# A gated DeltaNet and Conformer block: two sigmoids queued behind a rounding, and decay exponentials moved up in ScalarE's order

## The chip, the cores and the metric

The kernel runs on one core of one Trainium2 chip. The metric is the device time of one execution in microseconds (us). Each engine of the core (TensorE for matrix products, VectorE, ScalarE, GpSimd, and SyncE, which here issues the loads) works through a stream of instructions of its own in a fixed order; engines wait for one another by semaphores. In the profile they are called PE, DVE, ACT, POOL and SP, in that order; DMA is the transfer of data to and from HBM.

## The reference, cut to what matters

The block takes x of 512 tokens by 1024 channels, in float32. What lies around the change is the start:

```python
h = rmsnorm(x, norm1_w)
proj = h @ w_in                       # q, k, v, z, b, a, glu, gates
beta = sigmoid(b);  g = -exp(A_log) * softplus(a + dt_bias)
qkv = silu(causal_depthwise_conv(qkv, dn_conv_w))      # 4 taps
# per head and chunk of 64 tokens: gc = cumsum(g)
decay = exp(where(tril, gc[i] - gc[j], -inf))          # used twice per head
t_mat = eye + where(strict, beta[i] * (k @ k.T) * decay, 0)
attn = (q @ k.T) * decay
ga, gb = split(glu + b_glu);  c = ga * sigmoid(gb)     # then a 31-tap convolution
```

Behind that come the triangular solves and the recurrence over chunks, the merging of both mixers by sigmoid gates, a SwiGLU channel mixer and a last RMSNorm.

## The kernel before

**Tiling.** Channels lie on 128 partitions, tokens (512) along a row. A projection `proj(j)` (L397) gives 128 output channels: one weight unit of 128 x 1024 is loaded, ScalarE rounds it into `whi` (L113), VectorE subtracts to get the rest `wlo` (L115), and TensorE makes 8 x 3 products of 128 x 512 (L124): `whi` with `hh`, `whi` with `hl`, `wlo` with `hh`, where `hh` and `hl` are the rounded part and the rest of the normalized input, in 8 slices k. Raw weights, `whi` and `wlo` have three buffers each.

**The start.** While the norm is not yet known, the products of the first two pairs of gated units (win rows 40, 32, 41, 33) are made from the unnormalized input (L264 to L324). `normalized(k)` (L337) then makes slice k: VectorE scales `xt`, ScalarE rounds to `hh[k]` (L340), VectorE subtracts to `hl[k]` (L341). `glu0(i)` (L323) scales the early products, and its inner function `gated` does the sigmoid on ScalarE (L332) and the gating product on VectorE (L333). The small chain for g and beta stands between, with two Exp (L363, L364) and a Ln (L366). The first projections that use all 8 slices are those of k and q of head 0, interleaved (`proj2`, L408); so TensorE needs `hh[7]` and `hl[7]` last.

**The decays.** `decays` (L792) makes the cumulated sums of g on TensorE (L798), writes them to HBM (`mrow`, L809), and `masked` (L442) reads for each head a row broadcast into a tile `DT` (L446) and adds the triangular mask on GpSimd (L448). There are four `DT` buffers. `decay` (L453) then does four Exp of 128 x 128 for each head on ScalarE (L458). It is called in heads 0, 1, 3 and 5, for the heads (0, 1), (2, 3), (4, 5) and (6, 7). Users of a `DT` are `Un` x `DT` on GpSimd (L485) and `at` on VectorE (L523).

**What sets the order.** Each engine's stream is laid out when the program is built, by a list planner with a model of time: when an engine of the model falls free, it takes, of the instructions whose inputs and buffers are ready, the one with the lowest number. An instruction's number is the value of a counter (`tc.cur_priority`) that goes up by one with each instruction that the Python code emits. `tc.issue_after(i)` adds an order edge, only for instructions on the same engine as `i`, and no wait for `i` to end. In `decay` the first `issue_after` names a GpSimd instruction, so it binds no Exp; for the first call, `silu[0]` does. Activation-table loads (`ACT_TABLE_LOAD` in the profile) are not written by hand; they stand where the next function needs another table.

Counted through the code, ScalarE's instructions around the change have these numbers: Exp of the decays of heads 0 and 1 436 to 443; the copy that starts `y` (L504) 465; rounding of units 24, 42, 34, 9, 1, 17 (L113) 497, 525, 574, 589, 621, 653, of head 2's k, q and v 909, 957, 997; Silu of z (L844) 523; the four scalings of `Vp` (L518) 543 to 546; four squares (L526) from 556; the sigmoid of the third gated unit (L684) 572; Exp of the decays of heads 2 and 3 661 to 668; of heads 4 and 5 1397 to 1404; of heads 6 and 7 2164 to 2171. `hh[7]` (L340) has 274, the Ln (L366) 263, the two sigmoids (L332) 279 and 281. The masks of heads 2 and 3 on GpSimd (L448) have 445 and 447, `Un` x `DT` of head 0 (L485) 448. Unit 9 is k of head 1, the next projection behind unit 34.

Of the kernel before, what the change touches and what calls it, by code (L numbers as in the profile page):

```python
# [9 lines left out]
AF = mybir.ActivationFunctionType  # L10
# [14 lines left out]
START = 78  # L25
ROUND = 40
WARM = 9
OTHERS = (12, 12, 12, 12, 8, 8, 8, 8)
EPS = 1e-6

# [2 lines left out]
def block_kernel(ctx, tc, a):  # L33
    nc = tc.nc
    V, S, G, PE = nc.vector, nc.scalar, nc.gpsimd, nc.tensor
# [41 lines left out]
    hh = hp.tile([P, KD, T], F32R, name="hh")  # L77
# [138 lines left out]
    with tc.tile_pool(name="st", bufs=2) as st:  # L216
# [3 lines left out]
        xt = st.tile([P, KD, T], F32, name="xt", bufs=1)  # L220
# [28 lines left out]
        prio = tc.cur_priority  # L249
# [10 lines left out]
        wps = psg.tile([P, T], F32, name="g")  # L260
        for i in range(WARM):
            PE.matmul(wps, warm.broadcast_to([P, P]), warm.broadcast_to([P, T]), start=True, stop=True)
# [60 lines left out]
        def glu0(i):  # L323
            sg = tp.tile([P, T], F32, name="sg")  # L324
            V.tensor_tensor(out=sg, in0=eps_[2 * i], in1=rsb, op=ALU.mult)
            c = tp.tile([P, T + 30], F32, name="c", bufs=3)
            V.memset(c[:, 0:30], 0.0)
            V.tensor_tensor(out=c[:, 30:], in0=eps_[2 * i + 1], in1=rsb, op=ALU.mult)
            cs.append(c)

            def gated():
                S.activation(sg, sg, AF.Sigmoid, bias=b_glu[:, 8 + i:9 + i])  # L332
                V.scalar_tensor_tensor(out=c[:, 30:], in0=c[:, 30:], scalar=b_glu[:, i:i + 1], in1=sg,  # L333
                                       op0=ALU.add, op1=ALU.mult)
            return gated

        def normalized(k):  # L337
            V.scalar_tensor_tensor(out=xt[:, k, :], in0=xt[:, k, :], scalar=vec[:, k:k + 1], in1=rsb,
                                   op0=ALU.mult, op1=ALU.mult)
            S.activation(hh[:, k, :], xt[:, k, :], AF.Copy)  # L340
            V.tensor_tensor(out=hl[:, k, :], in0=xt[:, k, :], in1=hh[:, k, :].bitcast(F32), op=ALU.subtract)  # L341

        for k in range(2):
            normalized(k)
        gated = [glu0(0)]
        for k in range(2, 4):
            normalized(k)
# [17 lines left out]
        V.tensor_scalar(out=u, in0=t0, scalar1=1.0, scalar2=None, op0=ALU.add)  # L365
        ln_ = S.activation(sp, u, AF.Ln)  # L366
        for k in range(4, KD):
            normalized(k)
        gated.append(glu0(1))
        with tc.issue_after(ln_.ins):  # L370
            for g_ in gated:
                g_()

# [78 lines left out]

    def decay():  # L453

        with tc.issue_after(raised[-1][2].ins), nullcontext() if done else tc.issue_after(silu[0].ins):
            for h, DT, _ in raised:
                for n in range(NT):
                    S.activation(DT[:, n, :], DT[:, n, :], AF.Exp, bias=nmc[:, n, h:h + 1])  # L458
        raised.clear()

    def front(h, kT, DT):
        sq = junk[:, 0:P]
# [329 lines left out]
    def decays():  # L792

        yield 2
        gps = psg.tile([P, 4, P], F32, name="g")
        fl = lambda t: t.rearrange("p n h -> p (n h)")
        for i, m in enumerate((tri, suf, ones, mid)):
            PE.matmul(gps[:, i, 0:32], m, fl(g), start=True, stop=True)  # L798
        S.activation(fl(egc), gps[:, 0, 0:32], AF.Exp)
        S.activation(fl(kdf), gps[:, 1, 0:32], AF.Exp)  # L800
        S.activation(fl(egl), gps[:, 2, 0:32], AF.Exp)
        V.tensor_scalar(out=negc, in0=egc, scalar1=-1.0, scalar2=None, op0=ALU.mult)
        V.tensor_scalar(out=fl(nmc), in0=gps[:, 3, 0:32], scalar1=-1.0, scalar2=None, op0=ALU.mult)
        mps = psg.tile([P, 4, P], F32, name="g")
        PE.matmul(mps[0:32, 0, :], fl(g), mid, start=True, stop=True)
        mr = mrt[0:32, 0:P]
        S.activation(mr, mps[0:32, 0, :], AF.Copy)
        for n in range(NT):
            nc.sync.dma_start(mrow[:, n, :], mr[n * H:(n + 1) * H])  # L809
        masked(0, 1)  # L810

    def head(h, done):

        pk, pq = (yield from proj2()) if h == 0 else (None, None)
        k_ = yield from conv4(8 + h, "kT", pk)
        close()
        q_ = yield from conv4(h, "qT", pq)
        close()
        v = conv4(16 + h, "vT")
        for _ in range(2):  # L820
            next(v)
            yield
        DT = dts.pop(0)
        opening = front(h, k_, DT)
        if h == 0:
            with behind():
                next(opening)
            v_ = yield from v
        if raised:
            decay()  # L830
        if h % 2 == 0 and h + 2 < H:
            masked(h + 2, h + 3)
        with behind(), tc.issue_after(last[0].ins) if h else nullcontext():
            if h:
                next(opening)
            try:
                next(opening)
            except StopIteration as made:
                ss, kd, b2, Un, cp, y = made.value
        if h:  # L840
            v_ = yield from v
        pz = yield from proj(24 + h)
        z_ = zall[:, h, :]
        S.activation(z_, pz, AF.Silu)  # L844


        def second():
            Vp, at = front2(k_, q_, v_, DT, ss)
            done.append((h, k_, q_, ss, kd, b2, Un, cp, Vp, at, y, z_))
            yield 0  # L850

        chains.append([count[0] + 5, second()])
        yield
# [6 lines left out]
    def take(n):  # L860
        for _ in range(n):
            if next(rest, 0) == 0:
                return
            yield


    silu, raised, done, ended, dts, convs, count, chains = [None], [], [], [], [], [], [0], [[0, decays()]]
    rest = others()
    for h in range(H):
        queue.append(head(h, done))  # L870
        queue.append(take(OTHERS[h]))
    queue.append(rest)
    nh = 0
    while step() or chains:
        ahead[0] = count[0] >= 72
        start_feed[0] = count[0] >= 335
        if nh < H and count[0] >= START - 9 + 32 * nh + sum(OTHERS[:nh]):
            chains.append([0, chain(*done[nh])])
# [556 lines left out]
```

## Time and profile before

| | us |
|---|---|
| three runs | 934.72, 934.75, 937.58; median 934.75 |
| the profiled execution | 939.53 |
| its span, first to last instruction | 937.8 |
| busy in it: TensorE, VectorE, ScalarE, GpSimd | 920.3, 766.0, 567.6, 354.4 |

A row of a timeline reads: start (us from the span's start), length, engine, line, operation, what is written and read, how often; in brackets the time that the engine stood idle before it and what ended that. A row of the windows reads: stretch, its length, busy time of PE, PEld (weight loads), DVE, ACT and POOL with their counts, then the granted TensorE clock, the share of the DMA engines and GB/s. A product of 128 x 512 is shown with its whole length of 0.39 us, but the next one starts about 0.23 us after it, since they are pipelined.

### The profile page before, as it was taken

What the parts mean: (1) busy time and instruction counts of PE and PEld (TensorE: products, weight loads), DVE (VectorE), ACT (ScalarE), POOL (GpSimd) and SP (SyncE); (2) the same over time, 40 slices, a digit from 0 to 9 for tenths busy, and PEclk for the clock granted to TensorE, in tenths of its full rate; (3) what the DMA queues carried; (4) which work ended last, traced back from release to release, by engine and by line L of the source; (5) the groups of instructions that cost most, each with busy time, mean ns of one, the idle gap of its engine ahead of it and who ended that gap; (6) DMA issues with size and microseconds to landing.
All of it is one profiled execution on the core that took longest, in us unless ns stands there. A gap on an engine that the chain in (4) does not pass through costs nothing.

```text
span 937.8 us, 15306 instructions
## 1 busy us (share of the span) xinstructions
PE 920.3 (98%) x5204; PEld 793.4 (85%) x5204; DVE 766.0 (82%) x1207; ACT 567.6 (61%) x1295; POOL 354.4 (38%) x572
## 2 busy tenths in 40 slices
PE   9999999999999999999999999999999999999997
PEld 6778788888888888888888888889999999988886
DVE  4889898989989889999587543786787888889896
ACT  6687877898778796633565323454554444456545
POOL 0145366362654338534064252211033234133042
PEclk9999999999999999999999999999999999999999
DMA  9335766565755646988999998688677767577654
GB/s 309 127 113 180 183 181 157 141 188 114 184 137 149 166 112 198 309 251 270 277 283 302 289 262 213 195 212 250 214 258 243 264 214 258 183 241 253 211 183 154
DMA packets 90286, 197.62 MB, mean 211 GB/s; under 512 B 11424, under 2 KB 20816, under 8 KB 89184
## 3 DMA queue, kind: packets, MB, share of 16 engines
q1 hardware_dynamic: 75168, 161.93, 51.0%
q0 software_dynamic: 13744, 32.05, 17.8%
q10 hardware_dynamic: 1296, 2.67, 0.7%
q8 instruction: 41, 0.67, 0.3%
q14 instruction: 37, 0.30, 0.1%
HBM read 176.40 MB, written 60.05 MB: 252 GB/s over the span
## 4 chain that ended last, share of the span: by engine, by line
PE 76%; ACT 8%; DVE 6%; DMA 3%; issue 2%; SPq 0%; POOL 0%; POOLq 0%; ACTq 0%; DVEq 0%
PE mm L124 47%; PE w L124 23%; DVE wlo L115 3%; PE b L532 2%; ACT whi L113 2%; DMA raw<-s 2%; PE st L645 1%; DMA raw<-in_wgu_dram 1%; PE g L439 1%; DMA DT<-mrow 1%; PE st L636 1%; DVE acc L426 1%; PE st L644 0%; PE g L480 0%; ACT s L550 0%
## 5 line engine op out<-in xcount | busy, mean ns | idle before, releaser
L113 ACT ACTIVATE whi<-raw 128x1024 fp32r<-128x1024 f32 (+1 forms) x205 | 207.9, 1016 | 213.5 <-PE mm L124 112.1
L115 DVE TENSOR_TENSOR wlo<-raw,whi 128x1024 fp32r<-128x1024 f32 (+1 forms) x205 | 256.9, 1254 | 72.8 <-ACT whi L113 71.5
L124 PE MATMUL mm<-hh,whi 128*128 128x512 f32 (+1 forms) x612 | 236.1, 387 | 0.6 <-ACT hh L340 0.3
L124 PE MATMUL mm<-hh,wlo 128*128 128x512 f32 (+1 forms) x612 | 230.9, 378 | 0.0
L124 PE MATMUL mm<-hl,whi 128*128 128x512 f32 (+1 forms) x612 | 230.2, 376 | 0.0
L700 DVE SCALAR_TENSOR_TENSOR cps<-c,c31w,cps 128x512 f32<-128x512 f32 x224 | 167.9, 750 | 3.6
L124 PEld LDWEIGHTS mm<-hh,wlo 128*128 128x128 f32 x612 | 115.9, 189 | 19.0
L124 PEld LDWEIGHTS mm<-hh,whi 128*128 128x128 f32 x612 | 116.1, 190 | 17.5 <-ACT hh L340 0.8
L124 PEld LDWEIGHTS mm<-hl,whi 128*128 128x128 f32 x612 | 116.2, 190 | 16.2
L200 POOL DMA_DIRECT2D s<-s x38 | 32.7, 860 | 103.7 <-DMA s<-in_wgu_dram 95.8
L124 PE MATMUL w<-hh,wlo 128*128 128x256 f32 x244 | 69.2, 284 | 2.0 <-DVE wlo L115 2.0
L124 PE MATMUL w<-hh,whi 128*128 128x256 f32 x244 | 69.2, 284 | 0.1
L124 PE MATMUL w<-hl,whi 128*128 128x256 f32 x244 | 69.1, 283 | 0.0
L200 POOL DMA_DIRECT2D s<-in_wgu_dram x38 | 32.9, 873 | 90.9 <-DMA s<-in_wgu_dram 85.7
L1070 POOL TENSOR_TENSOR fm<-fm 128x256 f32<-128x256 f32 x33 | 31.9, 967 | 75.5 <-DVE s L1070 51.6
L426 DVE SCALAR_TENSOR_TENSOR acc<-mm,c4w,acc 128x511 f32<-128x511 f32 (+2 forms) x72 | 53.1, 742 | 3.0 <-ACT acc L423 2.9
L508 POOL TENSOR_TENSOR ytm<-U,y 128x60 f32<-128x60 f32 (+14 forms) x120 | 35.2, 293 | 47.2 <-DMA U<-sc 39.0
L176 POOL TENSOR_TENSOR wst<-wst 128x512 f32<-128x512 f32 x16 | 26.4, 1653 | 68.6 <-DMA wst<-in_wdn_dram 37.4
L124 PE MATMUL mm<-yl,whi 128*128 128x512 f32 x128 | 49.8, 389 | 0.0
L124 PE MATMUL mm<-yh,wlo 128*128 128x512 f32 x128 | 49.8, 389 | 0.0
L124 PE MATMUL mm<-yh,whi 128*128 128x512 f32 x128 | 49.8, 389 | 0.0
L124 PEld LDWEIGHTS w<-hh,wlo 128*128 128x128 f32 x244 | 46.8, 192 | 2.6 <-DVE wlo L115 2.6
(346 smaller groups left out, 2149.7 us busy)
## 6 DMA issues: line engine op xcount, KB each, us to landing
raw<-in_win_dram SPq DMA_DIRECT2D x61, 512.0 KB, 4.6
s<-in_wgu_dram SPq DMA_DIRECT2D x76, 256.0 KB, 5.1
raw<-s SPq DMA_DIRECT2D x76, 256.0 KB, 4.1
raw<-in_wgu_dram SPq DMA_DIRECT2D x25, 512.0 KB, 4.3
raw<-wsum SPq DMA_DIRECT2D x44, 256.0 KB, 4.1
s<-in_wgu_dram POOLq DMA_DIRECT2D x38, 256.0 KB, 5.7
s<-s POOLq DMA_DIRECT2D x38, 256.0 KB, 5.6
raw<-in_wdn_dram SPq DMA_DIRECT2D x33, 256.0 KB, 3.5
```

Source lines behind the costliest of these rows:

```text
L113: marked(S.activation(hi, raw, AF.Copy), "unit")
L115: marked(V.tensor_tensor(out=lo, in0=raw, in1=hi.bitcast(F32), op=ALU.subtract), "unit")
L124: marked(PE.matmul(ps, l, r, start=first and i == 0, stop=last and i == 2))
L176: G.tensor_tensor(out=o, in0=x, in1=y, op=ALU.add)
L200: fed.append(nc.gpsimd.dma_start(*begun.pop(0), accum_op=ALU.add, max_dma_last_dim=2048))
L426: marked(V.scalar_tensor_tensor(out=acc[:, s:], in0=ps[:, :T - s], scalar=c4w[:, j, k:k + 1], in1=acc[:, s:], op0=ALU.mult, op1=ALU.add))
L439: PE.transpose(ps[:, n, :], src[:, n, :], ident)
L508: G.tensor_tensor(out=tm[:, :, 0:w], in0=U[:, k, :, k + 1:], in1=y[:, :, k:k + 1].broadcast_to([P, NT, w]), op=ALU.mult)
L532: PE.matmul(ps[:, q, 0:w], stationary[:, q, :], moving[:, q, :], start=True, stop=True)
L636: PE.matmul(ps[:, 1, :], Y[:, n % 2 * 2 + n // 2, :], R, start=True, stop=True)
L700: V.scalar_tensor_tensor(out=acc if k < 30 else cv[i], in0=c[:, k:k + T], scalar=c31w[:, i, k:k + 1], in1=acc if k > 1 else cv[i], op0=ALU ...
L1070: return eng.tensor_tensor(out=out, in0=in0, in1=in1, op=op)
```

## The change

Two edits. `normalized` returns its rounding instruction, and the sigmoids of the first two gated units, so far queued only behind the Ln, are queued behind the rounding of slice 7 as well. In `decay`, the counter is set 200 lower while the Exp are emitted, for all calls but the first (`done` is empty only then), and set back to its old value after, in the first call too, so that what is emitted behind a call has numbers lower by 8 than before. Counted so, the Exp of heads 2 and 3 get 453 to 460 (the counter stands at 653 there, 8 lower than before), those of heads 4 and 5 1181 to 1188, those of heads 6 and 7 1940 to 1947; of the others behind the first call, the copy of `y` gets 457, Silu of z 515, `Vp` from 535, the sigmoid of the third unit 564, the rounding of unit 9 581.

```diff
+URGENT = 200
...
         def normalized(k):
...
-            S.activation(hh[:, k, :], xt[:, k, :], AF.Copy)
+            r = S.activation(hh[:, k, :], xt[:, k, :], AF.Copy)
             V.tensor_tensor(out=hl[:, k, :], in0=xt[:, k, :], in1=hh[:, k, :].bitcast(F32), op=ALU.subtract)
+            return r
...
         for k in range(4, KD):
-            normalized(k)
+            n_ = normalized(k)
         gated.append(glu0(1))
-        with tc.issue_after(ln_.ins):
+        with tc.issue_after(ln_.ins), tc.issue_after(n_.ins):
             for g_ in gated:
                 g_()
...
     def decay():
 
+        prio = tc.cur_priority
+        tc.cur_priority = prio - (URGENT if done else 0)
         with tc.issue_after(raised[-1][2].ins), nullcontext() if done else tc.issue_after(silu[0].ins):
             for h, DT, _ in raised:
                 for n in range(NT):
                     S.activation(DT[:, n, :], DT[:, n, :], AF.Exp, bias=nmc[:, n, h:h + 1])
         raised.clear()
+        tc.cur_priority = prio
```

## The prediction

> **What bounds the kernel now.** I read the page first, then the busy time by stages around the lines that the change touches, then the chain of waits up to 80 us.
>
> ```profile
> PE 920.3 (98%) x5204; PEld 793.4 (85%) x5204; DVE 766.0 (82%) x1207; ACT 567.6 (61%) x1295; POOL 354.4 (38%) x572
> ```
> ```profile
> 34.00:44.00 10.00, 9.66 (x43) 7.72 (x42) 9.13 (x21) 7.06 (x12) 0.00 (x0) 1.00 0.02 5
> 44.00:61.00 17.00, 17.00 (x85) 14.11 (x85) 14.99 (x31) 13.19 (x29) 2.64 (x9) 1.00 0.50 149
> 61.00:74.00 13.00, 11.90 (x59) 9.35 (x58) 11.21 (x15) 12.84 (x33) 9.64 (x13) 1.00 0.19 69
> 74.00:96.00 22.00, 22.00 (x104) 18.34 (x103) 20.74 (x29) 15.71 (x36) 15.04 (x35) 1.00 0.65 202
> 96.00:120.00 24.00, 21.94 (x106) 17.40 (x105) 19.97 (x38) 20.52 (x65) 9.03 (x15) 0.93 0.74 192
> ```
>
> TensorE is busy for 98% of the span, so a microsecond counts when TensorE stands still for it, and hardly otherwise. In the stages, TensorE misses 0.34 us from 34 to 44, nothing from 44 to 61, 1.1 us from 61 to 74, where ScalarE is full (12.84 of 13.00), nothing from 74 to 96, where ScalarE has 6.3 us to spare, and 2.1 us from 96 to 120. The change works at two places of this: at 43 us, and in ScalarE's full stretch up to 74.
>
> ```profile
> 43.78 6.44 PE mm L124 x27
> 50.22 0.82 PE g L798 x8
> ...
> 73.67 6.43 PE mm L124 x27
> ```
>
> The chain of waits runs from TensorE's products at 43.78 to the cumulated sums (L798), over the decays' transfer and ScalarE (left out here), and back to TensorE at 73.67. So what is won at 43.78 arrives at 73.67, and what ScalarE gets to do more in between is paid there.
>
> **The change, part by part.**
>
> *The two sigmoids.* ScalarE and TensorE at 40 us:
>
> ```profile
> 39.66 1.28 ACT L366 ACT_TABLE_LOAD   x1
> 40.96 0.23 ACT L366 ACTIVATE cv<-cv 128x32 f32<-128x32 f32 x1
> 41.19 1.28 ACT L332 ACT_TABLE_LOAD   x1
> 42.49 0.72 ACT L332 ACTIVATE sg<-sg,vec 128x512 f32<-128x512 f32 x1
> 43.12 0.61 ACT L340 ACTIVATE hh<-xt 128x512 fp32r<-128x512 f32 x1
> ```
> ```profile
> 43.06 0.39 PE L124 MATMUL mm<-hh,wlo 128*128 128x512 f32 x1
> 43.78 0.97 PE L124 MATMUL mm<-hh,whi 128*128 128x512 f32 x3 [0.34 <-ACT hh L340]
> 44.59 0.40 PE L124 MATMUL mm<-hl,whi 128*128 128x512 f32 x1
> ```
>
> The last slice's rounding stands behind the sigmoid table's load and one sigmoid, and TensorE waits for it. Put ahead of both, it starts where that load starts now, at 41.19, and ends at 41.8. A product takes a step of 0.24 us (27 in 6.44), so TensorE's next one would start at 43.30 instead of 43.78: 0.48 us won. The three products before the first `hl` took 0.81 (to 44.59) instead of 0.72: 0.09 more. For the subtraction on VectorE that makes `hl` there would be 2.2 us, from 41.8 to 44.0; now it is through 0.86 us behind the rounding (43.73 to 44.59). The gain is 0.6 us; its bounds are the 0.34 us shown as idle and 0.6. Nothing is added: one load, two sigmoids and one rounding change places, so the second sigmoid ends when it does now, and the first 0.6 us later. VectorE's gating products wait for that, and behind them the 31-tap convolutions, which is background work. The cumulated sums at 50.22 follow in TensorE's order, and nothing in the chain up to 73.67 is shown to be held by anything but its own start, so I carry the 0.6 us through.
>
> *The Exp of heads 2 and 3.* ScalarE, GpSimd, VectorE and TensorE from 61 to 80 us:
>
> ```profile
> 63.69 2.19 ACT L458 ACTIVATE DT<-DT,sm 128x128 f32<-128x128 f32 x7
> 65.79 0.23 ACT L504 COPY y<-cst 128x64 f32<-128x64 f32 x1
> 66.03 1.28 ACT L844 ACT_TABLE_LOAD   x1
> ...
> 71.36 1.06 ACT L113 ACTIVATE whi<-raw 128x1024 fp32r<-128x1024 f32 x1
> ...
> 73.75 1.07 ACT L113 ACTIVATE whi<-raw 128x1024 fp32r<-128x1024 f32 x1
> 74.84 1.28 ACT L458 ACT_TABLE_LOAD   x1
> 76.14 3.33 ACT L458 ACTIVATE DT<-DT,sm 128x128 f32<-128x128 f32 x11
> ```
> ```profile
> 63.30 3.79 POOL L448 TENSOR_TENSOR DT<-DT,cst 128x512 f32<-128x512 f32 x3
> ...
> 75.17 2.07 POOL L448 TENSOR_TENSOR DT<-DT,cst 128x512 f32<-128x512 f32 x1 [4.08 <-DMA DT<-mrow]
> ```
> ```profile
> 72.46 3.63 DVE L115 TENSOR_TENSOR wlo<-raw,whi 128x1024 fp32r<-128x1024 f32 x3 [0.33 <-ACT whi L113]
> ```
> ```profile
> 73.67 0.50 PE L124 MATMUL mm<-hh,whi 128*128 128x512 f32 x1 [0.21 <-ACT whi L113]
> 74.01 0.39 PE L124 MATMUL mm<-hl,whi 128*128 128x512 f32 x1
> 74.24 0.40 PE L124 MATMUL mm<-hh,wlo 128*128 128x512 f32 x1
> ```
>
> Now the Exp of heads 2 and 3 come at 76.14, behind the three roundings at 71.36 to 74.8 (units 9, 1 and 17). That is their rank by number, 661 against 653. Their masks were ready long before: the three at 63.30 are those of heads 1, 2 and 3, and end by 67.1. With 453 to 460 they outrank the Silu (515), `Vp`, the squares, the sigmoid (564) and the rounding of unit 9 (581), and follow the first eight Exp. So eight Exp move from a place where ScalarE has time to one where it has none. Each costs 3.33 / 11 = 0.30 us, together 2.4 us. The mask of head 3 ends at 67.1, when the Exp of head 2 are through, so no wait comes on top. Queued behind them are the Silu, `Vp`, the squares, the sigmoid, and unit 9: its rounding goes from 71.36 to 73.8 and ends at 74.8, its subtraction (3.63 / 3 = 1.21 us) ends at 76.1, where TensorE wants it now at 74.24, after two products. The cost is 76.1 - 74.24 = 1.9 us of TensorE's time; its bounds are 0, if the planner leaves the Exp where they are, and 2.4 us, if no slack is left. I take 1.9, by the rows of this very unit.
>
> The table load at 74.84 isn't saved. The row with eleven Exp holds the first of head 4 as well, whose mask was added at 75.17 and couldn't be earlier (it needs a buffer of head 0 and waited for its transfer); they stay and keep the load. So loads in all stay as they were, if heads 2 and 3 stay together with 0 and 1.
>
> *The Exp of heads 4 to 7.* From 1397 to 1181 and from 2164 to 1940.
>
> ```profile
> 118.46 1.28 ACT L458 ACT_TABLE_LOAD   x1
> 119.75 1.28 ACT L458 ACTIVATE DT<-DT,sm 128x128 f32<-128x128 f32 x4
> ```
>
> Head 5's ran at 119.75 amid head 2's work, with numbers from 909 to 997, so only because nothing more urgent was ready; with 1185 to 1188 they are still last in rank, and stay. The same goes for head 4 at 79 and heads 6 and 7. I cost these at nothing, and if one is drawn ahead of a rounding, at most the 2.6 us of load and Exp in these rows. The cover is the lead of the roundings: at 73.75 that of unit 17 ran while TensorE began unit 9, two units earlier.
>
> The sum: -0.6 + 1.9 = **+1.3 us**. The profiled execution took 939.53, 4.8 us more than the median of 934.75, so its own time would be 940.8; the difference carried to the median gives 934.75 + 1.3 = **936.1**.
>
> **The rivals.**
>
> *The clock drops at the new stall (slower).* What a stall of TensorE costs beyond itself shows at 105 us:
>
> ```profile
> 105.36 0.59 PE L532 MATMUL b<-m,s 128*128 128x16 f32 x4 [1.83 <-DVE m L568]
> ```
> ```profile
> 103.60:107.00 3.40, 1.64 (x11) 1.45 (x12) 3.08 (x4) 2.01 (x9) 3.11 (x7) 1.00 0.63 93
> 107.00:110.40 3.40, 3.40 (x10) 2.59 (x10) 3.24 (x9) 2.84 (x13) 0.79 (x3) 0.53 0.26 72
> ```
>
> After 1.83 us of idle time, with 1.64 of 3.40 us busy, the granted clock stood at 0.53 for the next 3.4 us, which lost 0.47 x 3.4 = 1.6 us. The 1.1 us missing from 61 to 74 cost no clock (1.00 there). The new stall is 1.4 us up to unit 9's rounding (74.85 against 73.45), two products, and 0.8 us up to its subtraction: 2.2 us idle in 2.7. If 1.8 us of that fall into one such stretch of 3.4, the clock drops: 936.1 + 1.6 = **937.7**, which is +0.31%. The Trainium skill (TensorE: Matmul & The Clock Gate, HAM oscillation) asks for no idle gap of over about 3.4 us, by which neither stall would drop the clock and 936.1 would stand; the rows at 105 disagree, with 1.83 us. Its Part 1 says the window is free-running, so whether a stall is met can differ by execution; one trace cannot show that.
>
> *The Exp are split.* If the planner puts the Silu between the Exp of head 2 and of head 3, ScalarE loads Exp's table once more, 1.28 us: **937.4**. By the Trainium skill (ScalarE: Activation LUTs, What ACT_TABLE_LOAD costs) a switch has a drain of about 1.38 us too, which would make it 938.8; the trace shows none: the copy at 65.79 ends at 66.02, the load starts at 66.03.
>
> *The Exp do not come earlier.* If in the planner's time the masks are late, or ScalarE has room there, only the first edit counts: 934.75 - 0.6 = **934.2**. Against it: GpSimd's order puts these masks ahead of head 0's `Un` product.
>
> *The stall at 105 us goes.* All of head 0's chain shifts against GpSimd and the transfers; if the 1.83 us and the dropped clock behind it go, 936.1 - 1.8 - 1.6 = **932.7**, and with the rival before, 930.8. Nothing in the edit aims at it, but it hangs on the planner's order alone.
>
> **How the numbers follow.** The forecast gets 0.36 (its own range, from the bounds of both terms, 934.2 to 936.8), the dropped clock 0.22, the split 0.12 (part of it with a dropped clock, 939.0), the Exp that stay 0.16, the stall that goes 0.14. A measurement of this kernel can tell about 0.3% from no change, here 2.8 us: below 931.9 or above 937.6. Faster by that needs two rivals together: 0.10. Slower takes half of the dropped clock and of the split: 0.24. Within: 0.66. The range leaves out the outer parts of the first and last rival: 932.6 to 939.0.
>
> **What would show it.** In the changed profile: ScalarE's last `hh` (L340) ahead of the sigmoids' table load, and no wait of TensorE for it near 43; eight more Exp in one piece before the Silu's load (L844) near 66, and only head 4's left near 77; the rounding of unit 9 some 2 us later against the Exp of heads 0 and 1, and a wait of TensorE of 1.5 to 2.2 us near 73; the table loads unchanged in number. It is wrong if that wait is missing, if TensorE's idle time elsewhere differs by more than 1.5 us, or if a granted clock of about half appears or goes.

## The result and the profile after

The changed kernel takes 945.28 us (median of 5 runs, 943.42 to 946.57), the kernel before 935.04 beside it (5 runs, 934.72 to 937.58): a ratio of 1.0101, with a 95% interval of 1.0086 to 1.0116. The forecast was 936.1 with a range up to 939.0; the change is slower, and by far more than any of the cases allowed. A repeat (the last experiment below) gave +0.67% (0.43 to 0.91), so the size differs somewhat, the sign doesn't. The profiled execution of the changed kernel took 946.57 us, its span is 7.0 us longer than that of before (937.8).

Line numbers of the changed file are 1 to 5 higher: the rounding is L114, the subtraction L116, the product L125, the last slice's `hh` L341, the Exp L462, the `Un` scalings L488, `Vp` L523, Silu of z L849. The page of the changed kernel:

```profile
span 944.8 us, 15313 instructions
...
PE 921.7 (98%) x5204; PEld 793.2 (84%) x5204; DVE 768.9 (81%) x1207; ACT 567.8 (60%) x1294; POOL 356.1 (38%) x572
```

TensorE's busy time grew by 1.4 us only (from 920.3), so the other 5.6 of the 7.0 are time in which it stood still. The same stages of the changed kernel as in the prediction, and two behind them:

```profile
34.00:44.00 10.00, 10.00 (x46) 8.29 (x45) 9.23 (x21) 7.34 (x12) 1.57 (x6) 1.00 0.00 0
44.00:61.00 17.00, 17.00 (x90) 14.21 (x89) 15.33 (x32) 14.86 (x35) 3.88 (x7) 1.00 0.57 179
61.00:74.00 13.00, 12.26 (x58) 9.62 (x58) 12.38 (x16) 12.94 (x35) 8.62 (x12) 1.00 0.22 67
74.00:96.00 22.00, 22.00 (x105) 18.35 (x104) 20.68 (x35) 12.94 (x30) 13.01 (x34) 1.00 0.68 201
96.00:120.00 24.00, 21.26 (x109) 16.86 (x108) 20.01 (x33) 21.49 (x68) 10.94 (x21) 1.00 0.68 179
120.00:173.00 53.00, 52.05 (x282) 43.42 (x281) 46.30 (x90) 37.55 (x119) 30.98 (x70) 1.00 0.63 157
173.00:200.00 27.00, 22.22 (x114) 17.60 (x113) 21.79 (x46) 22.70 (x79) 14.98 (x31) 0.94 0.38 102
```

and the last of these in the kernel before:

```profile
173.00:200.00 27.00, 26.80 (x144) 21.72 (x143) 24.03 (x51) 24.33 (x84) 13.46 (x28) 1.00 0.57 148
```

Up to 96 us nothing was lost: TensorE is now full from 34 to 61, and from 61 to 74 it misses 0.74 us where it missed 1.1. The loss lies some 110 us behind the edits. From 173 to 200 TensorE stood still for 4.78 us against 0.20, which is 4.58 of the 5.6 (behind 200 us there are 1.2 more), and the granted clock fell to 0.94 on top. That is 0.06 x 27 = 1.6 us of clock, about what the kernel before lost from 96 to 120 (0.07 x 24 = 1.7), where the changed kernel stays at 1.00; between these two profiles the clock evens out, and the 5.6 us of standing still make up most of the difference.

What happened there, on TensorE of the changed kernel:

```profile
190.54 0.40 PE L125 MATMUL mm<-hh,wlo 128*128 128x512 f32 x1
194.40 0.50 PE L125 MATMUL mm<-hh,whi 128*128 128x512 f32 x1 [3.46 <-ACT whi L114]
...
195.94 0.63 PE L125 MATMUL mm<-hl,whi 128*128 128x512 f32 x1
```
```profile
196.00:198.00 2.00, 2.00 (x7) 1.69 (x6) 1.41 (x3) 1.10 (x3) 1.76 (x4) 0.50 0.65 217
```

It waits 3.46 us for the rounding of a weight unit, unit 12 (k of head 4, the next projection). The products behind that are shown with 0.63 us instead of 0.40, and the granted clock from 196 to 198 is 0.50. ScalarE of the changed kernel:

```profile
176.66 1.14 ACT L488 ACTIVATE Un<-g,ss 128x128 f32<-128x128 f32 x4 [1.39 <-DVE ss L480]
...
192.05 1.22 ACT L603 COPY Y<-YY 32x128 f32<-32x128 f32 x4
193.29 2.95 ACT L114 ACTIVATE whi<-raw 128x1024 fp32r<-128x1024 f32 x3
```

and of the kernel before:

```profile
177.41 1.06 ACT L113 ACTIVATE whi<-raw 128x1024 fp32r<-128x1024 f32 x1 [2.07 <-PE mm L124]
178.37 1.12 ACT L483 ACTIVATE Un<-g,ss 128x128 f32<-128x128 f32 x4
...
188.98 1.06 ACT L113 ACTIVATE whi<-raw 128x1024 fp32r<-128x1024 f32 x1
...
196.49 1.05 ACT L113 ACTIVATE whi<-raw 128x1024 fp32r<-128x1024 f32 x1
```

Before, the rounding of unit 12 stood at 177.41, ahead of the four `Un` scalings, those of head 4's q and v at 188.98 and 196.49. After, the scalings come at once, then some 14 us of other work, most of it small steps of a head's chain, down to the copies into `Y`, and only then, from 193.29, all three roundings in a row. The edits name none of these instructions. By number the rounding always ranked behind those copies (1677 in the kernel before, the copies 1665 to 1668). So in the old layout the planner must have had a gap in its time where the rounding was the only one ready, and none in the new one; this is read from the numbers, not tested.

### The profile page after: what moved, and what is told of

It is laid out like the page before. It is cut to its first block, busy times and chain, and to the rows that moved or that the text cites. A ratio compares the mean times of both kernels' runs of the same rounds, so it can differ in the third digit from the quotient of the medians.

```text
span 944.8 us, 15313 instructions
## 1 busy us (share of the span) xinstructions
PE 921.7 (98%) x5204; PEld 793.2 (84%) x5204; DVE 768.9 (81%) x1207; ACT 567.8 (60%) x1294; POOL 356.1 (38%) x572
## 4 chain that ended last, share of the span: by engine, by line
PE 67%; ACT 10%; DVE 9%; issue 5%; DMA 5%; POOL 3%; SPq 1%; POOLq 0%; ACTq 0%; DVEq 0%
PE mm L125 40%; PE w L125 21%; DVE wlo L116 4%; DMA raw<-s 3%; ACT whi L114 2%; PE b L537 1%; DVE cw L1075 1%; DMA s<-in_wgu_dram 1%; POOL ytm L513 1%; PE g L441 1%; PE st L650 1%; DVE sacc L747 1%; PE b L125 1%; ACT DT L462 1%; PE st L649 1%
## 5 line engine op out<-in xcount | busy, mean ns | idle before, releaser
L114 ACT ACTIVATE whi<-raw 128x1024 fp32r<-128x1024 f32 (+1 forms) x205 | 207.7, 1015 | 209.0 <-PE mm L125 109.5
L116 DVE TENSOR_TENSOR wlo<-raw,whi 128x1024 fp32r<-128x1024 f32 (+1 forms) x205 | 254.0, 1239 | 75.6 <-ACT whi L114 71.7
L125 PE MATMUL mm<-hh,whi 128*128 128x512 f32 (+1 forms) x612 | 236.9, 387 | 4.7 <-ACT whi L114 4.7
L125 PE MATMUL mm<-hl,whi 128*128 128x512 f32 (+1 forms) x612 | 230.5, 377 | 0.0
L125 PE MATMUL mm<-hh,wlo 128*128 128x512 f32 (+1 forms) x612 | 230.1, 376 | 0.0
L125 PEld LDWEIGHTS mm<-hh,whi 128*128 128x128 f32 x612 | 116.1, 190 | 22.7 <-ACT whi L114 6.9
L125 PEld LDWEIGHTS mm<-hh,wlo 128*128 128x128 f32 x612 | 115.8, 189 | 19.2
L125 PEld LDWEIGHTS mm<-hl,whi 128*128 128x128 f32 x612 | 116.2, 190 | 15.9 <-issue 0.2
L125 PE MATMUL w<-hh,wlo 128*128 128x256 f32 x244 | 69.2, 284 | 1.5 <-DVE wlo L116 1.5
L125 PE MATMUL w<-hh,whi 128*128 128x256 f32 x244 | 69.1, 283 | 0.0
L125 PE MATMUL w<-hl,whi 128*128 128x256 f32 x244 | 69.0, 283 | 0.0
L513 POOL TENSOR_TENSOR ytm<-U,y 128x60 f32<-128x60 f32 (+14 forms) x120 | 42.1, 351 | 64.1 <-DMA U<-sc 42.1
L1075 POOL TENSOR_TENSOR fm<-fm 128x256 f32<-128x256 f32 x33 | 34.6, 1049 | 73.2 <-DVE s L1075 51.8
L125 PE MATMUL mm<-yl,whi 128*128 128x512 f32 x128 | 49.8, 389 | 0.0
L125 PE MATMUL mm<-yh,whi 128*128 128x512 f32 x128 | 49.8, 389 | 0.0
L125 PE MATMUL mm<-yh,wlo 128*128 128x512 f32 x128 | 49.8, 389 | 0.0
L125 PEld LDWEIGHTS w<-hh,wlo 128*128 128x128 f32 x244 | 46.7, 192 | 2.1 <-DVE wlo L116 2.1
```

The source lines that it names most:

```text
L114: marked(S.activation(hi, raw, AF.Copy), "unit")
L116: marked(V.tensor_tensor(out=lo, in0=raw, in1=hi.bitcast(F32), op=ALU.subtract), "unit")
L125: marked(PE.matmul(ps, l, r, start=first and i == 0, stop=last and i == 2))
L513: G.tensor_tensor(out=tm[:, :, 0:w], in0=U[:, k, :, k + 1:], in1=y[:, :, k:k + 1].broadcast_to([P, NT, w]), op=ALU.mult)
L1075: return eng.tensor_tensor(out=out, in0=in0, in1=in1, op=op)
```

## The experiments

Two theories. **R**: the loss is the new place of unit 12's rounding, a by-product of laying out the order anew. **E**: the loss is what the moved sigmoids and Exp themselves cost, near 43 and 74 us. The kernels have the line numbers of before. A ratio is to the kernel before, run on the same chip; it comes from the runs of both and isn't the quotient of the two medians (for the second edit alone that would be 1.0066 instead of 1.0050). Where a kernel has both edits, they are left out of the diff.

**Each edit alone.** The first only (sigmoids behind the rounding of slice 7):

> First edit alone (the sigmoids behind the last rounding). Theory R (the loss comes from one rounding, that of unit 12, k of head 4, which in the changed kernel stands behind head 2's chain on ScalarE): here that rounding stands ahead of head 3's Un scalings, as in the kernel before, so no long wait of TensorE near 190 us and a time of 932 to 936. Theory E (the Exp and sigmoids that were moved cost the time where they now stand): 934 to 936, since the eight Exp are not moved. So this one alone parts only from a third theory, that any change of the start costs about 10 us by disturbing all that follows: 940 or more.

935.89 us against 936.16, ratio 1.0000 (0.9987 to 1.0012). Its windows:

```profile
34.00:44.00 10.00, 10.00 (x46) 8.29 (x45) 9.23 (x21) 7.04 (x12) 0.89 (x3) 1.00 0.00 0
173.00:200.00 27.00, 26.60 (x144) 21.74 (x143) 23.53 (x50) 24.74 (x79) 15.00 (x35) 1.00 0.58 160
```

The wait at 43 is gone, as forecast, and from 173 to 200 it is no worse than before by more than 0.2 us (26.60 against 26.80). The 0.6 us forecast is 0.06%, half of what the interval can tell, so the gain is neither shown nor excluded.

The second only (Exp behind the first call 200 lower):

> Second edit alone (the higher rank of the Exp of heads 2 and 3; the others do not move in ScalarE's order). Theory R: the rounding of unit 12 stands ahead of the Un scalings here too, so 934 to 938, and no wait near 190 us. Theory E: the eight Exp in ScalarE's full stretch cost most of what the changed kernel lost: 942 or more.

942.31 us against 936.16, ratio 1.0050 (1.0030 to 1.0070): R's number missed, E's met. Its windows and its TensorE:

```profile
61.00:74.00 13.00, 11.33 (x58) 9.20 (x58) 12.31 (x18) 12.94 (x38) 8.46 (x13) 1.00 0.21 71
74.00:96.00 22.00, 21.14 (x91) 16.89 (x91) 20.38 (x25) 12.95 (x27) 13.49 (x34) 0.92 0.62 174
```
```profile
73.81 0.50 PE L124 MATMUL mm<-hh,whi 128*128 128x512 f32 x1 [1.67 <-ACT whi L113]
...
75.01 0.50 PE L124 MATMUL mm<-hh,whi 128*128 128x512 f32 x1 [0.47 <-ACT whi L113]
...
76.13 0.80 PE L124 MATMUL mm<-hh,wlo 128*128 128x512 f32 x1 [0.38 <-DVE wlo L115]
76.72 0.63 PE L124 MATMUL mm<-hh,whi 128*128 128x512 f32 x1
```

This is the prediction's second term and its first rival, close in size: waits of 1.67, 0.47 and 0.38 us for unit 9's rounding, the next one and a subtraction, 2.5 us in all where 2.2 were forecast, then products of 0.63 us, and a clock of 0.92 from 74 to 96, which is 0.08 x 22 = 1.8 us where 1.6 were forecast. Unit 12 is not late here (rounded at 177.91). So by itself the second edit does cost what E says; it just isn't what the two edits together did, where only 0.27 and 0.47 us of these waits are left (shown further below).

**Unit 12's rounding, put in and taken away.** The kernel before, with neither edit, but with this rounding behind the copies into `Y`:

```diff
-        marked(S.activation(hi, raw, AF.Copy), "unit")
+        with tc.issue_after(ycopy[0].ins) if rush[0] == 12 else nullcontext(): marked(S.activation(hi, raw, AF.Copy), "unit")
...
-        hi, lo = unit(a["win"][j])
+        rush[0] = j; hi, lo = unit(a["win"][j]); rush[0] = None
...
-            S.copy(out=Y[b, :, b], in_=YY[b])
+            ycopy[0] = S.copy(out=Y[b, :, b], in_=YY[b])
```

> The kernel before, with neither edit, but the rounding of unit 12 queued behind the last copy into Y of head 2's chain, so that the roundings of units 12, 4 and 20 stand in one block as in the changed kernel. Theory R: a wait of TensorE of 3 us or more near 190 us, and about 5 us more than before: 938.5 to 941.5. Theory E: no change, 934 to 936.

944.2 us, ratio 1.0078 (1.0059 to 1.0097): E's number missed, and R's 938.5 to 941.5 too, since the loss is larger than forecast. Its ScalarE, TensorE and a window:

```profile
192.41 2.95 ACT L113 ACTIVATE whi<-raw 128x1024 fp32r<-128x1024 f32 x3
```
```profile
193.53 0.50 PE L124 MATMUL mm<-hh,whi 128*128 128x512 f32 x1 [3.21 <-ACT whi L113]
```
```profile
173.00:200.00 27.00, 22.43 (x113) 17.65 (x112) 21.71 (x47) 22.29 (x75) 14.75 (x30) 0.94 0.40 113
```

The same block of three roundings, nearly the same wait (3.21 us against 3.46), the same clock, and a loss of 0.78% between the 0.67 and the 1.01 of the changed kernel, without a line of the change. The other way round, both edits with unit 12's rounding and subtraction 300 lower:

```diff
+        d_ = 300 if rush[0] in (12,) else 0; tc.cur_priority -= d_; marked(S.activation(hi, raw, AF.Copy), "unit")
...
+            marked(V.tensor_tensor(out=lo, in0=raw, in1=hi.bitcast(F32), op=ALU.subtract), "unit"); tc.cur_priority += d_
```

> Both edits, and the rounding and the rest of unit 12 with a rank 300 higher, which puts that rounding among head 3's Un scalings again; the order up to there is that of the changed kernel. Theory R: the wait of 3.5 us near 191 and the 3.4 us of half clock behind it go, that is 5 us: 938.5 to 941.5. Theory E: nothing of the moved work is undone: 944 to 947. A third, that ScalarE is simply overfull there: the wait only moves to a chain step, and 943 to 947.

939.1 us, ratio 1.0026 (1.0013 to 1.0039), as R has it.

```profile
175.45 1.06 ACT L113 ACTIVATE whi<-raw 128x1024 fp32r<-128x1024 f32 x1
```
```profile
173.00:200.00 27.00, 26.11 (x140) 21.15 (x139) 23.62 (x51) 23.88 (x80) 14.97 (x30) 1.00 0.50 131
```

Most of the loss (0.75 of 1.01 points, or 0.41 of the 0.67 of the repeat) goes with this one rank, and so does the stop: 26.11 of 27 us and a clock of 1.00. Both directions together show R for the main part. 0.26% stays. The clocks of the single runs say the same, beyond the profiled ones: the mean granted clock is 0.994 to 0.997 in all eleven runs of the changed kernel and 0.992 to 0.997 with unit 12 late, but 0.998 in the median of the kernel before (65 runs beside the experiments) and of both edits with unit 12 early.

**Is the 200 at fault?** With 100, and with 250, in its place:

> Both edits with 100 in place of 200. The Exp of heads 2 and 3 still come right behind those of heads 0 and 1 and Vp, but the planner leaves the rounding of unit 12 ahead of head 3's Un scalings. Theory R: no wait of 3 us near 190, 935 to 940. The rival that the moved Exp themselves cost it: 943 to 947, as with 200.

> Both edits with 250 in place of 200. ScalarE does the Exp of heads 0 to 3 in one piece as with 200, but the planner puts the rounding of unit 12 behind Vp, between its place in the kernel before (ahead of Un) and that in the changed one (behind the copies into Y). Theory R: that is some 5 us ahead of the block of three and ahead of TensorE's need near 191, so no wait of 3 us there, 936 to 940. The rival that the moved Exp cost the time: 943 to 947.

With 100, unit 12 is rounded at 173.62, ahead of the scalings, and the time is 938.17 us, ratio 1.0019 (1.0004 to 1.0035), as R has it. With 250 it is rounded in between:

```profile
188.11 1.07 ACT L113 ACTIVATE whi<-raw 128x1024 fp32r<-128x1024 f32 x1
```
```profile
61.00:74.00 13.00, 10.36 (x53) 8.19 (x51) 9.74 (x14) 10.73 (x29) 9.77 (x13) 1.00 0.17 63
173.00:200.00 27.00, 26.84 (x147) 22.63 (x147) 24.69 (x52) 24.91 (x86) 14.63 (x30) 1.00 0.39 109
```

Only 0.16 us are missing from 173 to 200, and the 940.47 us (1.0039, 1.0020 to 1.0059; half a us above R's range) go with 2.64 us missing from 61 to 74, 1.90 of them a wait for VectorE at 69.17 that no other kernel here has. A number chosen for eight Exp decides through the layout where TensorE stops next, and it isn't a matter of more or less.

**The second edit, with units 9 and 12 raised by 200 and 300.** The first is the unit on which exp_only waits.

```diff
+        d_ = {9: 200, 12: 300}.get(rush[0], 0); tc.cur_priority -= d_; marked(S.activation(hi, raw, AF.Copy), "unit")
```

> The second edit alone, with the roundings of unit 9 (rank 200 higher, so that it stands ahead of all the decays' Exp) and of unit 12 (300 higher, so that it stays where it is in the kernel before). The second edit alone cost +0.50%, with 2.5 us of waits of TensorE from 73 to 77 and a granted clock of 0.92 from 74 to 96. Theory R (a rounding that TensorE needs next must not stand behind work that can wait): these waits and the lost clock go, 935 to 938. The rival, that eight Exp in a full stretch cost their time whatever stands first: the wait moves to another step of the same stretch, 940 to 943.

940.17 us, ratio 1.0033 (1.0022 to 1.0045): R's number missed, the rival's met. The waits aimed at are gone:

```profile
61.00:74.00 13.00, 13.00 (x66) 10.63 (x65) 12.13 (x18) 12.93 (x37) 9.42 (x13) 1.00 0.30 94
```

and so is the lost clock (1.00 from 74 to 96), but part at most of the time came back (the interval overlaps that of exp_only); other waits stand at 95.35 (0.78 us) and 102.77 (1.15), behind the stretch in which the rival looked for them.

**Would roundings first be the cure?** All projections' roundings and subtractions, 200 lower with both edits and 100 lower with the first edit alone, by the diff above with `rush[0] is not None` as its condition:

> Both edits, and the roundings and rests of all units of the first part with a rank 200 higher, so that no rounding stands behind head chains that were written down earlier. Theory R in its general form: under 937, perhaps under the kernel before, 931 to 937. The rival, that the chain steps now wait behind roundings and TensorE for them: 938 or more.

> The first edit alone, and the roundings and rests of all units of the first part with a rank 100 higher. Theory R in its general form: 930 to 936, at or under the kernel before. The rival, that chain steps wait instead: 938 or more.

944.45 us (1.0098, 1.0077 to 1.0120) and 947.09 (1.0101, 1.0076 to 1.0127): R's numbers missed, the rival's met. The waits that lead on TensorE, first in the one with both edits (what waited for what: us in total, times, longest):

```profile
PE b L532 <- ACT m L585: 2.3, 1, 2.3
```

and in the other:

```profile
PE b L532 <- ACT m L585: 5.2, 1, 5.2
```

Now TensorE waits for a small step of the chain (the copy into `m`, L585). What stands ahead of that step on ScalarE, again first with both edits:

```profile
146.07 1.28 ACT L458 ACT_TABLE_LOAD   x1 [2.92 <-DMA DT<-mrow]
```
```profile
145.69 1.28 ACT L458 ACT_TABLE_LOAD   x1 [6.23 <-DMA DT<-mrow]
```

It isn't a rounding in the main: the copy stands behind an Exp of a later head's decay, and ScalarE itself stands idle until that head's `DT` has been read from HBM, 2.92 and 6.23 us. VectorE had the copy's input ready by 144.3 and 140.2. With both edits one rounding of 1.06 us stands between as well; with the first edit alone none does. So the rival's numbers came out, but not its mechanism: raising the roundings laid out the order anew once more, and this time an instruction that waits for a transfer stands ahead of a chain step.

**The changed kernel once more:**

> The changed kernel once more (its instructions stand in the same order on every engine; only the source lines are laid out as in the kernel before), beside the next one on the same chip. Every theory: 943 to 947, with the wait of 3 us or more near 191.

944.0 us, ratio 1.0067 (1.0043 to 1.0091), with a wait of 3.47 us for the same rounding at 193.35. The place of the loss is the same in each profile.

## Why the prediction was wrong

*The sigmoids.* Right in the mechanism. ScalarE of the changed kernel:

```profile
40.30 0.62 ACT L341 ACTIVATE hh<-xt 128x512 fp32r<-128x512 f32 x1
40.93 1.28 ACT L333 ACT_TABLE_LOAD   x1
42.22 1.34 ACT L333 ACTIVATE sg<-sg,vec 128x512 f32<-128x512 f32 x2
```

The rounding stands ahead of the load, and TensorE's wait is gone (10.00 of 10.00). In time it can't be told from nothing (ratio 1.0000 alone).

*The Exp of heads 2 and 3.* Right in the kernel that has this edit alone, wrong in the one forecast. ScalarE and TensorE of the changed kernel:

```profile
58.41 0.64 ACT L849 ACTIVATE A<-mm 128x512 f32<-128x512 f32 x1
58.90 1.18 ACT L488 ACTIVATE Un<-g,ss 128x128 f32<-128x128 f32 x4
60.10 1.28 ACT L462 ACT_TABLE_LOAD   x1
61.39 4.80 ACT L462 ACTIVATE DT<-DT,sm 128x128 f32<-128x128 f32 x16
...
69.61 1.06 ACT L114 ACTIVATE whi<-raw 128x1024 fp32r<-128x1024 f32 x1
```
```profile
70.72 0.50 PE L125 MATMUL mm<-hh,whi 128*128 128x512 f32 x1 [0.27 <-ACT whi L114]
...
71.92 0.50 PE L125 MATMUL mm<-hh,whi 128*128 128x512 f32 x1 [0.47 <-ACT whi L114]
```

All sixteen Exp do stand in one block, as forecast. But the Silu and the `Un` scalings moved ahead of it, so that the Silu's own table load is gone (ScalarE has 1294 instructions, one fewer; the forecast had the loads unchanged), and unit 9's rounding comes at 69.61, not at 73.8. The wait of 1.9 us became 0.74, and the stage from 61 to 74 lost nothing by it (0.74 us missing, 1.1 before). The two edits don't add up. In time this is clear by the result only: 0.00% and 0.50% alone, 1.01% together, but 0.67% (0.43 to 0.91) in the repeat. It is clear by the place: together they lose from 173 to 200, where neither alone does (26.60 and 26.36 of 27 us busy).

*The Exp of heads 4 to 7.* Right: built with the lower counter for heads 2 and 3 alone, every engine's order is the same as in the changed kernel; built with it for heads 4 to 7 alone, the same as with the first edit alone.

*The step that failed* is the sum itself, "-0.6 + 1.9": two terms, each costed where its edit stands, and every instruction behind them left in its old place, at nothing. Where it did look further, at the Exp of heads 4 to 7, the cover that it named, "the lead of the roundings", was read at 73.75 and taken to hold behind that. The runs put in its place: a layout made anew from the edits on, in which one rounding of 1.06 us lost its gap some 110 us later, and with it 3.46 us of wait and some 1.6 us of clock (0.06 of 27 us), while the +1.9 was not paid in its place. The rivals had the same fault: all lie between 60 and 107 us. That the forecast, too, was slower is luck: the wait that it was added up from is not what made the kernel slower. The prediction's own test did catch it, idle time elsewhere that differs by more than 1.5 us, and a new half clock.

*The stall at 105 us* did not go in this profile, against the last rival, but no clock was lost behind it, so the stage of 96 to 120 came out better, not worse. First this profile, then that of the changed kernel's repeat, which has the same order on every engine:

```profile
103.61 0.59 PE L537 MATMUL b<-m,s 128*128 128x16 f32 x4 [2.15 <-DVE m L573]
```
```profile
102.72 0.59 PE L532 MATMUL b<-m,s 128*128 128x16 f32 x4 [0.50 <-DVE m L568]
```

2.15 and 0.50 us with the same order: this wait differs by execution, so that the 3.4 us which the last rival would have saved (1.83 of wait, 1.6 of clock) were those of one execution.

**What stays open.** The last 0.2 to 0.3% of the kernels with unit 12 early (1.0026, 1.0019) isn't pinned to a row: their profiles show several waits under 1 us, besides one of 1.2 for a subtraction and one of 1.69 at 103.17 (unit 12 early only), which have their like in the kernel before. The medians of the changed kernel and the one before differ by 10.2 us, the profiled spans by 7.0, since the profiled execution of before lies 4.5 us above its median; the split above is of the 7.0. Its granted clock is 0.996, where the 65 runs beside the experiments have 0.998 in the median; 0.002 x 938 = 1.9 us of the 4.5 may be that (an estimate from these two clocks), about what the half clock behind 105 us cost. Why the planner had no gap near 177 in the new layout was read from ranks, not tested. No version here beats the kernel before; the first edit alone equals it.

## What to carry to other kernels

Where a planner lays out each engine's stream, a changed rank is a change of the whole order behind it: cost it by comparing the order in which the two kernels are built, engine by engine, above all the instructions that feed the busiest engine, and widen the range where that can't be done. Two edits that are harmless or cheap alone may not add up. A rounding, a copy or any other feeder that ran early only because nothing else was ready has no claim on its place; where TensorE depends on it, a rank for its whole kind did not help here (+0.98% and +1.01%). An order edge for that one feeder is the next thing to try; no run here did.

## What the runs showed of the hardware

That a pause costs the clock was known from the row at 105 us; how little its length decides was not. The changed kernel around its wait of 2.15 us:

```profile
100.00:103.60 3.60, 1.46 (x9) 0.92 (x8) 2.82 (x4) 2.59 (x12) 2.22 (x3) 1.00 0.76 137
103.60:107.00 3.40, 3.39 (x19) 2.84 (x20) 2.96 (x9) 2.68 (x8) 2.21 (x7) 1.00 0.36 66
```

and the kernel with the second edit alone, ahead of and in the dropped clock:

```profile
73.10:76.50 3.40, 1.84 (x5) 0.97 (x6) 3.40 (x4) 3.38 (x8) 1.28 (x1) 0.90 0.37 116
76.50:79.90 3.40, 3.40 (x10) 2.65 (x10) 3.37 (x4) 2.95 (x6) 2.83 (x6) 0.60 0.76 202
```

With 1.46 of 3.60 us busy the clock stayed at 1.00, with 1.84 of 3.40 busy it fell, to 0.60 over the next 3.4. The wait at 105 us says the same: 1.83 us in the kernel before, with a clock of 0.53 behind it, but 2.15 here, 1.95 with unit 12 late and 1.69 with both edits and unit 12 early, each with a clock of 1.00 from 96 to 120. So it isn't the length of the pause or the idle time in such a stretch alone. That it is where the pause falls would fit, but no run varied that alone. The Trainium skill (TensorE: Matmul & The Clock Gate, Part 1) has a window of about 3.4 us that runs free of the kernel's own times, which fits these rows; its advice (HAM oscillation) to avoid idle gaps of over about 3.4 us does not, as gaps of at most 1.67 us were enough here.
